# Hybrid decoder layer: rotary rows of the second key tile loaded with the first head, the last two gate stores moved to ScalarE, and another count of transfers in the planner

## The chip, the cores and the metric

The kernel runs on one core of a Trainium2 chip. The metric is the time of one execution on the device, in microseconds; the median of three runs stands for a kernel. The core has TensorE (PE) for matrix products, VectorE (DVE), ScalarE (ACT) and GpSimd (POOL) for elementwise work, SyncE (SP), which only issues transfers here, and 16 DMA engines. Each engine works through its own instructions in the order in which they were emitted, and waits at an instruction whose semaphores are not there yet.

## The reference

One layer of a decoder with 1024 tokens, 16 learned meta tokens in front, and 1024 channels. Cut to its core:

```python
h = rms_norm(h_res, pre_norm_g)
z = h @ w_in                       # 1024 -> 7328 columns: all branches, their gates, four merge gates
y_a = (pool_mixer(...) * silu(pg)) @ w_out_pool
y_b = (mla_attention(cq, ckv, kr, ...) * silu(mg)) @ w_out_mla
y_c = (conformer_conv(...) * silu(cg)) @ w_out_conf
y_d = (short_conv(...) * silu(sg)) @ w_out_sc
gts = sigmoid(gl + gate_bias)      # four gates of 1024 channels per token
m = gts[0]*y_a + gts[1]*y_b + gts[2]*y_c + gts[3]*y_d
out = h_res + rms_norm(m @ w_o, post_norm_g)
```

Attention has 8 heads. A key has 64 components of its own head and 32 rotary components, which are the same for every head (`k_rope` is broadcast). Values have 64 components.

## The kernel before

**Three stages.** Stage one is the input projection (with the convolutions, the norms and the attention's low-rank projections woven in); it ends with the 32 tiles of merge gates, which are written to DRAM as `th0` to `th31`. Stage two is attention, 8 heads by 2 halves of the queries, with the products of the other three branches (`fills`) as filling work. Stage three is the attention's output product and the product with `w_o`. Every operand of a product is kept as a high and a low part, and each product is made of three.

**The planner.** The code doesn't issue instructions directly: `PE`, `ACT`, `DVE`, `POOL` and `SP` record operations in a `Plan`, and `flush` puts the operations of one stage in an order by simulating them with assumed costs. An operation is ready when its dependencies have ended; among the ready ones of an engine, the lowest `prio` goes first (its place in the recording, less what `ahead` adds; the filling products are recorded with `plan.ahead(-400)`, so they come 400 places later). `behind` makes operations wait, in the plan alone, until the product of TensorE that was recorded last has ended. The start of an operation on SP or ScalarE that is a transfer also needs `fits`: with eight or more transfers in the list `landed`, the eighth last must have landed. Transfers of POOL are not in that list. A buffer gets a slot when its first operation starts; the slots of stage two lie on memory that stage one used, and each is free only when its last user there is done.

**Flushes.** `flush` is called once for each stage, and emits its whole order before the next stage is recorded. Each engine goes on, in the plan, from where it stood: SP, whose last operation of stage one is early, plans stage two's loads from there.

**Completion of transfers.** In the built program the transfers that SP and ScalarE issue (622 in all) add to eight semaphores, in turn; before a transfer is issued, its engine waits until all earlier transfers on the same semaphore are complete, that is, also the one eight places ahead in the program. POOL's two transfers use other semaphores.

**The gate stores.** `out_gate(g)` makes two tiles of gates, `th{g}` and `th{g+1}`, and stores each with ScalarE; for the last pair, `g == 30`, with POOL.

**The start of stage two.** POOL makes the masks `maskS`, `maskT`, the tile `negd`, and row 96 to 99 of both key tiles `kt[0]` and `kt[1]`. Heads alternate between these two tiles and between `vt[0]` and `vt[1]`. `load_kv(h)` loads the 64 key rows of a head and its values; the 32 rotary rows go once into each tile, with head 0 into `kt[0]` and with head 1 into `kt[1]`. `maxima(h, c)` makes the scores once to take each query's maximum (VectorE adds the mask and reduces; the result goes into the query tile's rows 96 to 99), and `attend(h, c)` makes them again, transposed, with the maximum subtracted, for the exponential on ScalarE and the split on POOL, and then the product with the values. At the beginning `load_q(0, 0)`, `load_kv(0)`, `load_q(0, 1)` and the first maxima are recorded; then, for each unit `i`, under `plan.behind()`, the loads of the query after next and of the next head.

**Filling work.** Each filling product needs `bo` (a branch's output, two tiles), `whl` (weights) and, for its eviction, `th` (a gate tile).

Of the kernel before, what the change touches and what calls it, by code (L numbers as in the profile page):

```python
# [14 lines left out]

# [49 lines left out]
def f(ap):  # L65
    return ap.bitcast(F32)
# [127 lines left out]
class Plan:  # L194
# [139 lines left out]
    def flush(self):  # L334
# [26 lines left out]
        def slot(b, t):  # L361

            free = [sl for sl in b.group["slots"] if not sl["live"] and sl["after"] <= t]
            if free and (b.group["any"] or b.group["order"][b.group["next"]] is b):
                return min(free, key=lambda sl: (sl["after"], sl["i"]))

        def fits(o, t):

            if o["op"] == "dma_start" and o["eng"] != "POOL" and len(self.landed) >= 8 and self.landed[-8] > t:
                return False  # L370
            return all(slot(b, t) for b in o["bufs"] if not b.live and b.group)

        while events:
            t = events[0][0]
            while events and events[0][0] <= t:
                _, kind, i = heapq.heappop(events)
                if kind == 0:
                    o = self.ops[i]
                    bisect.insort(ready[o["eng"]], (o["prio"], o["i"]))
                elif kind == 2:  # L380
                    for b in self.ops[i]["bufs"]:
                        b.left -= 1
                        if b.left == 0 and b.group:
                            b.slot["live"], b.slot["after"] = None, t
            for e in self.free:
                if self.free[e] > t:
                    continue
                o = next((self.ops[i] for _, i in ready[e] if fits(self.ops[i], t)), None)
                if o is None:
                    if e == "PE" and self.idle and self.ops[self.idle[1]]["end"] is None:  # L390
                        order.append(self.idle[0])
                        self.free[e] = t + 160
                        heapq.heappush(events, (self.free[e], 1, 0))
                    continue
                ready[e].remove((o["prio"], o["i"]))
                for b in o["bufs"]:
                    if not b.live:
                        b.live = True
                        if b.group:
                            b.slot = slot(b, t)  # L400
                            b.slot["live"] = b
                            b.group["next"] += 1
                o["start"] = t
                if o["turns"]:
                    o["cost"] += max(0, self.port[{"DVE": "POOL", "POOL": "DVE"}[e]] - t) * 0.7
                    self.port[e] = t + o["cost"]
                self.free[e] = t + o["cost"]
                o["end"] = t + o["cost"] + self.WAKE[e]
                if o["op"] == "dma_start":
                    if self.pipe is None:  # L410
                        self.pipe = max((x["done"] for x in self.ops if x["op"] == "dma_start"
                                         and "done" in x and x["start"] <= t), default=0)
                    o["done"] = self.pipe = max(self.pipe, t) + o["bytes"]
                    land = self.pipe + o["bytes"] + 4500 + min(0, o["extra"])
                    o["end"] = land + max(0, o["extra"])
                    if o["eng"] != "POOL":
                        self.landed.append(land)
                    heapq.heappush(events, (land, 1, 0))
                for b in o["bufs"]:
                    b.last = max(b.last, o["end"])  # L420
                order.append(o)
                heapq.heappush(events, (self.free[e], 1, 0))
                heapq.heappush(events, (o["end"], 2, o["i"]))
                for u in o["users"]:
                    u["need"] -= 1
                    same = u["eng"] == e and o["op"] != "dma_start"
                    u["at"] = max(u["at"], self.free[e] if same else o["end"])
                    if not u["need"]:
                        heapq.heappush(events, (u["at"], 0, u["i"]))
# [8 lines left out]
def trunk_kernel(ctx, tc, a):  # L438
    nc = tc.nc
    plan = Plan(nc)  # L440
    PE, ACT, DVE, POOL, SP = (plan.engine(e) for e in ("PE", "ACT", "DVE", "POOL", "SP"))
# [7 lines left out]
    def ld(out, in_):  # L449
        SP.dma_start(f(out) if out.dtype == F32R else out, f(in_) if in_.dtype == F32R else in_)  # L450
# [38 lines left out]
    th_dram = [dram.tile([P, NT], F32, name=f"th{i}") for i in range(32)]  # L489
# [6 lines left out]
    kr_dram = dram.tile([32, 2, L], F32R, name="kr")  # L496
# [136 lines left out]
    def full(to, x, ps):  # L633

        if x is None:
            copy(to, ps)
        else:
            add(DVE, to, ps, x)

    def pairs_of_halves(n, each, store):  # L640

        z = {}

        def out(i, j, ps, x, tmp):
            first = i not in z
            if first:
                z[i] = up.tile([P, 2, n], F32, tag="z", bufs=2, name="z")
            m = ps.shape[0]
            each(i, z[i][:m, j], ps, x, tmp)
            if not first:  # L650
                store(i, z[i][:m])
        return out
# [11 lines left out]
    def row(t):  # L664
        return t.rearrange("p j n -> p (j n)")
# [16 lines left out]
    def out_gate(g):  # L682

        def each(i, to, ps, x, tmp):
            if x is not None:
                full(to, x, ps)
            ACT.activation(to, ps if x is None else to, AF.Tanh, scale=0.5,
                           bias=par[:, R_GB + g + i:R_GB + g + i + 1])
        return pairs_of_halves(512, each, lambda i, t: (POOL if g == 30 else ACT).dma_start(th_dram[g + i], row(t)))

# [587 lines left out]
    def load_q(h, c):  # L1280
        qt[h, c] = qk.tile([NA, 2, 512], F32R, tag="q", bufs=3, name="qt")
        ld(qt[h, c][:QK].rearrange("p s n -> p (s n)"), q_dram[c][h].rearrange("p s n -> p (s n)"))

    load_q(0, 0)
    kt = [qk.tile([NA, 2, L], F32R, name=f"kt{i}") for i in range(2)]
# [4 lines left out]
    def load_kv(h):  # L1290
        e, k_, v_ = h % 2, kt[h % 2], vt[h % 2]
        ld(k_[:64].rearrange("p s n -> p (s n)"), k_dram[h // 2][64 * e:64 * (e + 1)].rearrange("p s n -> p (s n)"))
        if h == 0:
            ld(k_[64:96], kr_dram)
        if h == 1:
            ld(k_[64:80], kr_dram[16:])
            ld(k_[80:96], kr_dram[:16])
        v = v_dram[h // 4][h % 4]
        ld(v_[:, 0:8].rearrange("p j c -> p (j c)"), v[:, 0:8].rearrange("p j c -> p (j c)"))
        ld(v_[:NM, 8], v[:NM, 8])  # L1300
# [91 lines left out]
    op, smg = {}, {}  # L1392
# [58 lines left out]
    def refill():  # L1451
        count["u"] += 1
        while count["f"] < min(48, 48 * count["u"] / (NUNIT - 2)):

            with plan.ahead(-400):
                next(fill, None)
            count["f"] += 1
# [9 lines left out]
    def lead_to(i, n=0):  # L1467

        while lead["i"] <= min(i, len(seq) - 1) or lead["steps"] < n:
            if next(steps, "end") == "end":  # L1470
                lead["steps"] = math.inf
            lead["steps"] += 1

    load_kv(0)
    load_q(*seq[1])
    lead_to(0)
    units = 0
    for i, (h, c) in enumerate(seq):
        with plan.behind():
            if i + 2 < len(seq):  # L1480
                load_q(*seq[i + 2])
            if c == 0 and h + 1 < H:
                load_kv(h + 1)
            if c == 0 and h % 2:
                smg[h] = at.tile([P, NT], F32, tag="smg", name="smg")
                ld(smg[h], z_dram[f"mg{h // 2}"])
        for _ in attend(h, c):
            units += 1
            lead_to(-1, min(5 + units * 10 / 14, 5 * (i + 3)))
            refill()  # L1490
        lead_to(i + 1)
        with plan.ahead(-300):
            if h == H - 1:
                head_out(h, c, sums_pe(h, c))
            elif c:
                for k, rb in enumerate(sums(h)):
                    head_out(h, k, rb)
# [82 lines left out]
    for d in (0, 4, 1, 5, 2, 6, 3, 7):  # L1580
# [3 lines left out]
        for c in range(2):  # L1584
            t = th[:, 512 * c:512 * (c + 1)]
# [23 lines left out]
    def half(name, bufs=4):  # L1609
        return ep.tile([P, 512], F32, tag=name, bufs=bufs, name=name)  # L1610
# [71 lines left out]
    for t in range(4):  # L1682

        parts = [slice(0, 512)] if t < 3 else [slice(0, 256), slice(256, 512)]
        g = half("g", 1) if t == 3 else a_[t]
# [45 lines left out]
```

## Time and profile before

| | us |
|---|---|
| median of three runs (1006.8 to 1009.5) | 1008.29 |
| profiled execution, time | 1008.78 |
| profiled execution, span | 1007.1 |
| TensorE busy | 983.7 |
| GpSimd busy | 688.1 |
| VectorE busy | 685.0 |
| ScalarE busy | 448.3 |

The mean granted clock of TensorE is 0.994. All operations have one line in the profile, that of the helper which issues them (L332), so groups are told apart by the names of their tiles: `ps_pa` to `ps_pd` are the projection, `ps_s` scores and maxima, `ps_o` the product with the values, `ps_y` the filling products, `ps_u` and `ps_o` late in the span the last stage. `SPq` and `ACTq` are the queues in which SP and ScalarE issue transfers; `PEclk` is the granted clock.

### The profile page before, as it was taken

How to read it: one execution, taken by the hardware profiler on the slowest of the kernel's cores; microseconds unless marked ns; L12 is line 12 of the kernel's file. 1: busy time of each engine (PE TensorE's matmuls, PEld its weight loads, DVE VectorE, ACT ScalarE, POOL GpSimd, SP SyncE). 2: the span in 40 equal slices, each digit the busy share in tenths (PEclk: the TensorE clock that was granted, in tenths of full speed). 3: DMA queues.
4: the chain of work that ended last, by engine and by line, in shares of the span. 5: the costliest groups of instructions: out<-in, count | busy, mean ns of one | idle time of the engine just before them, and what ended most of it. 6: DMA issues, size and time to landing. Idle time of an engine off the chain costs nothing.

```text
span 1007.1 us, 15176 instructions
## 1 busy us (share of the span) xinstructions
PE 983.7 (98%) x5091; PEld 826.2 (82%) x5091; DVE 685.0 (68%) x1106; ACT 448.3 (45%) x895; POOL 688.1 (68%) x640
## 2 busy tenths in 40 slices
PE   9999999999999999999999999989999999999996
PEld 8999898889888878887877888868887878688885
DVE  5855695997899499444455453266677698598747
ACT  7633234443444545444444444215664655424632
POOL 6767876766777668667777676124588785846956
PEclk9999999999999999999999999999999999999998
DMA  7268756678775865766655556895757771572634
GB/s 248 76 219 281 247 169 190 194 244 294 242 248 186 283 215 177 241 176 191 204 178 187 175 167 167 293 267 161 235 175 224 212 232 54 209 242 72 207 118 167
DMA packets 126302, 203.13 MB, mean 202 GB/s; under 512 B 19650, under 2 KB 79161, under 8 KB 124880
## 3 DMA queue, kind: packets, MB, share of 16 engines
q1 hardware_dynamic: 121600, 185.38, 58.6%
q10 hardware_dynamic: 4336, 15.73, 4.2%
q8 instruction: 40, 0.66, 0.3%
q0 software_dynamic: 288, 1.05, 0.3%
q14 instruction: 38, 0.31, 0.1%
HBM read 128.40 MB, written 73.72 MB: 201 GB/s over the span
## 4 chain that ended last, share of the span: by engine, by line
PE 90%; DVE 4%; issue 2%; POOL 2%; DMA 1%; ACT 0%; SPq 0%; DVEq 0%; POOLq 0%; ACTq 0%
PE ps_pa L332 16%; PE ps_pb L332 16%; PE ps_pc L332 15%; PE ps_o L332 9%; PE ps_pd L332 8%; PE ps_u L332 7%; PE ps_s L332 7%; PE ps_y L332 6%; PE ps_x L332 4%; PE ps_w L332 1%; DMA kt<-kr 1%; POOL pt L332 1%; DVE mx L332 1%; DVE a L332 1%; DVE op L332 0%
## 5 line engine op out<-in xcount | busy, mean ns | idle before, releaser
L332 PE MATMUL ps_pb<-T,S 128*128 128x512 f32 (+2 forms) x792 | 172.4, 362 | 0.8 <-DVE u L332 0.8
L332 PE MATMUL ps_pa<-B,A 128*128 128x512 f32 (+2 forms) x792 | 172.2, 362 | 0.0
L332 POOL TENSOR_TENSOR S<-ss,S 128x512 fp32r<-128x512 f32 x84 | 110.5, 1328 | 77.2 <-ACT S L332 77.0
L332 PEld LDWEIGHTS ps_pa<-B,A 128*128 128x128 f32 x792 | 134.6, 188 | 24.4 <-issue 0.5
L332 PEld LDWEIGHTS ps_pb<-T,S 128*128 128x128 f32 x792 | 133.8, 188 | 24.4 <-DVE u L332 1.2
L332 POOL TENSOR_TENSOR A<-raw,A 128x512 fp32r<-128x512 f32 x84 | 117.0, 1398 | 48.2 <-ACT A L332 42.2
L332 POOL TENSOR_TENSOR pt<-p,pt 128x512 fp32r<-128x512 f32 (+4 forms) x112 | 106.1, 976 | 41.6 <-ACT pt L332 27.8
L332 ACT ACTIVATE S<-ss 128x512 fp32r<-128x512 f32 x84 | 50.8, 628 | 115.7 <-DVE ss L332 73.0
L332 PE MATMUL ps_y<-bo,whl 128*128 128x512 f32 x288 | 87.9, 410 | 1.3 <-DVE th L332 1.3
L332 DVE SCALAR_TENSOR_TENSOR ps_w<-conv,par,ps_w 128x512 f32<-128x512 f32 x116 | 87.2, 752 | 2.4
L332 PE MATMUL ps_pc<-B,S 128*128 128x512 f32 (+2 forms) x396 | 87.5, 364 | 0.5 <-DVE z L332 0.5
L332 PE MATMUL ps_pc<-T,S 128*128 128x512 f32 (+2 forms) x396 | 86.4, 363 | 0.4 <-DVE z L332 0.4
L332 ACT ACTIVATE p<-ps_s 128x512 f32<-128x512 f32 (+4 forms) x112 | 49.9, 446 | 82.1 <-DVE ps_s L332 30.9
L332 PE MATMUL ps_pd<-T,A 128*128 128x512 f32 (+2 forms) x396 | 84.9, 361 | 0.0
L332 PEld LDWEIGHTS ps_pc<-T,S 128*128 128x128 f32 x396 | 67.1, 188 | 13.2 <-issue 1.0
L332 PEld LDWEIGHTS ps_pc<-B,S 128*128 128x128 f32 x396 | 66.9, 188 | 13.2 <-issue 1.0
L332 PE MATMUL ps_o<-pt,vt 128*128 128x512 f32 (+4 forms) x336 | 76.2, 332 | 0.8 <-POOL pt L332 0.6
L332 PEld LDWEIGHTS ps_pd<-T,A 128*128 128x128 f32 x396 | 66.9, 188 | 11.9
L332 PE MATMUL ps_s<-qt,kt 100*128 100x512 f32 (+4 forms) x336 | 71.9, 333 | 2.1 <-DVE qt L332 2.1
L332 ACT ACTIVATE A<-raw 128x512 fp32r<-128x512 f32 x84 | 52.7, 627 | 37.0 <-PE ps_pd L332 23.0
L332 PEld LDWEIGHTS ps_s<-qt,kt 100*128 100x128 f32 x336 | 56.6, 184 | 14.7 <-DVE qt L332 3.4
L332 PEld LDWEIGHTS ps_o<-pt,vt 128*128 128x128 f32 x336 | 52.7, 174 | 13.3 <-POOL pt L332 2.3
(344 smaller groups left out, 1895.1 us busy)
## 6 DMA issues: line engine op xcount, KB each, us to landing
raw<-in_w_in_dram SPq DMA_DIRECT2D x56, 512.0 KB
th<-th SPq DMA_DIRECT2D x32, 512.0 KB
th<-z ACTq DMA_DIRECT2D x30, 512.0 KB
v<-vhl SPq DMA_DIRECT2D x16, 384.0 KB
qt<-q SPq DMA_DIRECT2D x16, 384.0 KB
vt<-v SPq DMA_DIRECT2D x8, 768.0 KB
bo<-bo SPq DMA_DIRECT2D x6, 1024.0 KB
kt<-k SPq DMA_DIRECT2D x8, 520.0 KB
```

The costliest lines, as they stand in the source:

```text
L332: getattr(self.handle[o["eng"]], o["op"])(*map(real, o["args"]), **{k: real(v) for k, v in o["kw"].items()})
```

## The change

```diff
         def fits(o, t):
-            if o["op"] == "dma_start" and o["eng"] != "POOL" and len(self.landed) >= 8 and self.landed[-8] > t:
+            if o["op"] == "dma_start" and o["eng"] != "POOL" and sum(s <= t < e for s, e in self.landed[-40:]) >= 8:
                 return False
...
                     if o["eng"] != "POOL":
-                        self.landed.append(land)
+                        self.landed.append((t, land))
...
-        return pairs_of_halves(512, each, lambda i, t: (POOL if g == 30 else ACT).dma_start(th_dram[g + i], row(t)))
+        return pairs_of_halves(512, each, lambda i, t: ACT.dma_start(th_dram[g + i], row(t)))
...
         if h == 0:
             ld(k_[64:96], kr_dram)
-        if h == 1:
-            ld(k_[64:80], kr_dram[16:])
-            ld(k_[80:96], kr_dram[:16])
+            ld(kt[1][64:80], kr_dram[16:])
+            ld(kt[1][80:96], kr_dram[:16])
...
     for i, (h, c) in enumerate(seq):
-        with plan.behind():
+        with plan.behind() if i else nullcontext():
             if i + 2 < len(seq):
                 load_q(*seq[i + 2])
```

The limit of eight now counts the transfers that have started and not landed at the time in question, among the last 40. The stores of `th30` and `th31` are issued by ScalarE. The rotary rows of `kt[1]`, two transfers of 130 KB, are loaded in `load_kv(0)`. The loads that are recorded at the first unit, the query of head 1 and head 1's keys and values, no longer wait in the plan for the last recorded product.

More of the change, by code (lines that the diff above doesn't have):

```diff
@@ L13 @@
 import re
-from contextlib import ExitStack, contextmanager
+from contextlib import ExitStack, contextmanager, nullcontext
 import concourse.bass as bass
```

## The prediction

> **What bounds the kernel now.** I read the page first: TensorE is busy nearly the whole span, so a change can only give back, or take, time in which it idles or runs below full clock.
>
> ```profile
> PE 983.7 (98%) x5091; PEld 826.2 (82%) x5091; DVE 685.0 (68%) x1106; ACT 448.3 (45%) x895; POOL 688.1 (68%) x640
> ```
>
> 1007.1 - 983.7 leaves 23.4 us of idle. The change works at the join of projection and attention, so next comes the chain of waits there, and then the stretches around it.
>
> ```profile
> 653.23 10.28 PE ps_y L332 x44
> ...
> 666.42 10.27 DMA kt<-kr
> ```
>
> ```profile
> 660.00:670.00 10.00, 9.19 (x41) 7.04 (x41) 7.67 (x20) 0.00 (x0) 0.11 (x1) 1.00 0.91 266
> 670.00:680.00 10.00, 7.66 (x37) 6.17 (x36) 5.67 (x16) 4.38 (x11) 3.76 (x6) 0.84 0.96 248
> ```
>
> ```profile
> 676.00:678.00 2.00, 1.18 (x5) 1.21 (x6) 0.61 (x2) 0.00 (x0) 0.00 (x0) 0.71 1.06 376
> 678.00:680.00 2.00, 2.00 (x9) 1.69 (x9) 0.00 (x1) 0.60 (x1) 0.00 (x0) 0.50 0.77 154
> 680.00:682.00 2.00, 2.00 (x7) 1.62 (x6) 1.42 (x4) 0.00 (x0) 0.00 (x0) 0.50 0.19 70
> 682.00:684.00 2.00, 2.00 (x7) 1.57 (x6) 1.62 (x4) 0.00 (x0) 0.00 (x0) 0.58 0.00 0
> ```
>
> In the stretches the first number pair is TensorE; the last three numbers are granted clock, DMA share and GB/s. TensorE fills the start of attention with branch products (`ps_y`) and then waits for the second key tile's rotary rows. The idle time is 0.81 + 2.34 = 3.15 us. The clock loss is 2 x (0.29 + 0.50 + 0.50 + 0.42) = 3.4 us. So this join costs 6.6 us: the most that closing the hole can bring.
>
> Why does attention start late? The timelines of GpSimd, TensorE and VectorE:
>
> ```profile
> 633.10 1.29 POOL L332 TENSOR_TENSOR S<-ss,S 128x512 fp32r<-128x512 f32 x1 [1.48 <-ACT S L332]
> 650.76 0.77 POOL L332 DMA_DIRECT2D th<-z  x1 [16.38 <-ACT z L332]
> 653.55 0.54 POOL L332 DMA_DIRECT2D th<-z  x1 [2.02 <-ACT z L332]
> 654.08 0.22 POOL L332 MEMSET maskS<- 128x128 f32 x1
> ...
> 658.33 0.16 POOL L332 MEMSET mx<- 128x12 f32 x2
> ```
>
> ```profile
> 651.59 0.58 PE L332 MATMUL ps_s<-kt,qt 96*128 96x144 f32 x3
> 652.01 1.10 PE L332 MATMUL ps_y<-bo,whl 128*128 128x512 f32 x4
> ...
> 668.50 1.95 PE L332 MATMUL ps_s<-qt,kt 100*128 100x512 f32 x9 [0.34 <-DVE qt L332]
> ```
>
> ```profile
> 664.14 1.47 DVE L332 TENSOR_REDUCE mx<-ps_s 128x1 f32<-128x144 f32 x4
> ```
>
> GpSimd waits 16.4 us to issue the last two gate stores and only then builds the masks and clears `mx`. VectorE's maxima therefore come at 664.14, and the first scores with an exponent (100 rows) at 668.50. The branch products keep TensorE busy meanwhile, because their operands have landed by 652.01. That cover is what I ask about next. The timeline of the transfers, SyncE with ScalarE's two stores:
>
> ```profile
> 631.03 0.33 ACTq L332 DMA_DIRECT2D th<-z  x1
> 633.81 0.33 ACTq L332 DMA_DIRECT2D th<-z  x1
> ```
>
> ```profile
> 614.41 0.42 SPq L332 DMA_DIRECT2D qt<-q  x1
> 614.88 0.51 SPq L332 DMA_DIRECT2D kt<-k  x1
> 615.79 1.52 SPq L332 DMA_DIRECT2D kt<-kr  x1
> 619.07 0.30 SPq L332 DMA_DIRECT2D qt<-q  x1
> 631.64 1.02 SPq L332 DMA_DIRECT2D whl<-w_out_pool  x2
> ```
>
> ```profile
> 634.41 0.32 SPq L332 DMA_DIRECT2D vt<-v  x1
> ```
>
> ```profile
> 638.11 0.32 SPq L332 DMA_DIRECT2D vt<-v  x1
> 638.53 0.37 SPq L332 DMA_DIRECT2D bo<-bo  x1
> ```
>
> ```profile
> SPq L332 <- DMA th<-z: 4.6, 2, 3.4
> ```
>
> The last row is from the grouped waits of SyncE's queue between 612 and 640. A load of attention values has nothing to do with a gate store, and yet it waits for two of them. The reason is in the program: transfers of SyncE and ScalarE take eight completion semaphores in turn, and each waits until the one eight places ahead has landed. Loads 1 to 6 of the second stage went out by 632.7; load 7 (`vt`, 634.41) is eight places behind ScalarE's store of 631.03, load 8 (638.11) behind that of 633.81. So these stores held SyncE 3.4 and 4.3 us after their issue. GpSimd's last two stores use other semaphores and hold nobody.
>
> **The change part by part.** The sum is made against the profiled execution, span 1007.1 and time 1008.78 us, 0.5 above the median of 1008.29.
>
> 1. *Two stores to ScalarE.* ScalarE issues them for 2 x 0.33 us, with nothing behind it until the first exponential: cost 0. GpSimd loses its 16.38 us wait and can build masks from 634.4, where its last split ends. VectorE can then take the maxima when the first scores arrive, at about 653, and the exponent scores could come some 5 us later instead of at 668.50. That is the gain, if keys, values and branch operands are there. The price: the stores now take two of the turns, just before the second stage's loads. They go out at about 650.8 and 653.6 as before, because the activations that feed them don't move. With the 3.4 and 4.3 us above they land at about 654.5 and 657.5. Counted in turns, load 5 now waits for the store of 631.03 (634.4), load 6 for that of 633.81 (638.1), load 7 for about 654.5, and load 8 (or 9, if a load stands between the two stores) for about 657.5. SyncE is one queue: whatever is behind them waits too.
>
> 2. *Transfers counted by their times.* The planner's old rule looked at the eighth last transfer in the list, landed or planned, and so held loads back as the turns do. The new one counts only those already started. It lets the planner put more loads ahead on paper; the turns don't follow the planner. Within a stage, where every listed transfer has started, both count nearly the same: 0, with 1 us either way for small shifts of order.
>
> 3. *Rotary rows early; no fence at the first unit.* Head 1's keys, values and queries get a place ahead of the branch loads, since the branch loads have 400 added to their order. Sizes from the transfers' view:
>
> ```profile
> bo<-bo SPq DMA_DIRECT2D x6, 1024.0 KB
> ...
> vt<-v SPq DMA_DIRECT2D x8, 768.0 KB
> ```
>
> Two queries, keys and rotary rows of both heads make about eight loads, whose buffers are free early. So the first values, the branch operands `bo` and the branch weights come at or behind load 9, that is after 657.5. Ahead of the second `bo`: values of two heads 2 x 780 KB, two weights 512 KB, two `bo` 2048 KB, in all 4120 KB or 4.2 MB. The rate of saturated stretches:
>
> ```profile
> 642.00:646.00 4.00, 4.00 (x19) 3.25 (x18) 1.38 (x2) 0.73 (x1) 0.00 (x0) 1.00 0.99 357
> 646.00:650.00 4.00, 4.00 (x19) 3.22 (x18) 0.69 (x1) 0.96 (x2) 0.00 (x0) 1.00 1.01 382
> ```
>
> At 370 GB/s this takes 11.4 us, plus about 2 us to land (3.4 us for a store of 0.52 MB, less 1.4 at that rate): 671. If `bo` stands right behind load 9, 2.1 MB need 5.7 + 2: 665.
>
> *The cover that is gone.* After the projection TensorE has three or four maxima products and then branch products: in the order of before the first `ps_y` is the fourth instruction, at 652.01. TensorE keeps its order, so from about 653 it stands at that product until 665 to 671: 12 to 18 us, and I take 15, between both positions of `bo`. All else of attention stands behind. Then it restarts at reduced clock: the row of before gives 3.4 us. By the Trainium skill (TensorE: Matmul & The Clock Gate, Part 1) half clock comes after an idle window of about 3.4 us and ends after as long a busy one, which would make the restart 1.7 us; the row above, half clock after a wait of 2.2 us, differs from it, and I keep the row. By the skill the sum below would be 1.7 us lower.
>
> *Given back later.* Fewer branch products are used up before the attention starts, so more are left to fill its later holes. The largest of these:
>
> ```profile
> 860.00:880.00 20.00, 17.58 (x86) 12.98 (x85) 10.46 (x16) 6.85 (x15) 15.69 (x14) 1.00 0.75 261
> ```
>
> It holds 2.42 us of idle; bounds 0 and 2.4, I take 0.6, as products were left there in before too.
>
> Sum: -6.6 (old hole) + 15 + 3.4 - 0.6 = +11.2, from 1008.78 to about 1020. Low end: -6.6 + 12 + 1.5 (restart within a shorter low-clock stretch) - 2.4 = +4.5, 1013. High end: -6.6 + 18 + 3.4 + 2 (gate tiles `th` come behind `bo` and hold evictions) = +16.8, 1025.6.
>
> **The rivals.**
>
> *The hole closes (faster).* If the second stage's loads take their turns before the two stores, or SyncE has all of its early loads out by then, nothing waits. For it: SyncE issued nothing between 619.4 and 631.6, and DMA stood still in part of that time:
>
> ```profile
> 626.00:630.00 4.00, 4.00 (x19) 3.26 (x18) 1.00 (x2) 1.76 (x4) 1.30 (x1) 1.00 0.02 6
> ```
>
> Against it: the stores belong to the stage that is emitted first, and in the program of before the first load stands between GpSimd's two stores, not ahead of both. Time: 1008.78 - 6.6 + 1 for new order = 1003. The Trainium skill says the same by another way (DMA: Bandwidth & Descriptors, "Issuing engines are not separate DMA queues"): all issuers share the DMA engines, and a change of issuer saves only issue time. No row of before contradicts that on the transfers; the wait of 4.6 us above lies in front of the issue, which the rule doesn't count.
>
> *SyncE is held, but the order on TensorE has attention first (about the same).* If scores of the first unit stand ahead of the first branch product, TensorE works on maxima and scores until about 658 and idles some 6 us until values land near 661 to 663. Then -6.6 + 6 + 3.4 - 1 = +1.8: 1010. Against it: in before a branch product follows the third maxima product. It decides between this and my forecast whether the planner believes in operands at 652, and it does.
>
> *The change does nothing at the join.* The loads' order is set by buffers that come free at 631 to 641, the rotary rows land early but another load is waited for. Then 1008. The count by times alone, without the turns, could do this. I give it little.
>
> **How the numbers follow.** SyncE held and TensorE standing at the first branch product: 0.66, time 1013 to 1026, likeliest 1020. Hole closes: 0.19, 1001 to 1005. SyncE held but covered: 0.10, 1006 to 1013. Nothing: 0.05, 1006 to 1010. What a measurement of this kernel can tell from no change is about 0.3%, 3 us: 1005.3 to 1011.3. Faster gets 0.19; same 0.11 (0.05, and most of the 0.10); slower 0.70. The range for 8 in 10 must reach below the likeliest case's own 1013 to 1026, through the middle cases and into the faster one: 1003 to 1026.
>
> **What would show it.** GpSimd's mask rows move to about 635, and the `th<-z` rows stand on ScalarE's queue at about 650.5 and 653.3: these I expect in any case. Held: SyncE's queue has a gap that ends at about 654 and 657 with the releaser `DMA th<-z`, and `bo<-bo` is issued after 657; DMA share falls to near zero between 642 and 650, where it was 0.99; TensorE idles over 10 us with the releaser `DMA bo<-bo` and the clock goes to 0.5. Wrong: `bo<-bo` still at about 638 to 641, exponent scores near 658, clock at 1.00 from 650 to 700; then the stores' turns came after the loads.

## The result and the profile after

The changed kernel takes 1024.45 us (median of 4 runs, 1023.62 to 1024.52), the kernel before beside it 1008.89 (1006.80 to 1012.09): ratio 1.0149, 95% interval 1.0121 to 1.0178. The profiled execution has a span of 1022.7 us, 15.6 more than before, and a mean clock of 0.984 instead of 0.994.

The page's row of busy times, of the changed kernel:

```profile
PE 986.8 (96%) x5091; PEld 829.4 (81%) x5091; DVE 683.3 (67%) x1106; ACT 446.6 (44%) x895; POOL 688.2 (67%) x638
```

The same 5091 products were busy for 3.1 us more, and 1022.7 - 986.8 = 35.9 us were idle instead of 23.4. So 12.5 us of the 15.6 are standing still; the other 3.1 are the same products running longer, and the mean clock fell with them. The stretches around the join show where (pairs in the order TensorE, weight loads, VectorE, ScalarE, GpSimd; then clock, DMA share, GB/s):

```profile
640.00:650.00 10.00, 10.00 (x45) 8.13 (x44) 2.08 (x3) 2.05 (x3) 0.16 (x2) 1.00 0.04 11
650.00:660.00 10.00, 1.80 (x9) 1.27 (x8) 2.63 (x7) 0.81 (x2) 0.00 (x0) 0.78 0.76 232
660.00:670.00 10.00, 1.49 (x3) 0.83 (x3) 0.00 (x0) 0.00 (x0) 0.00 (x0) 0.50 1.00 386
670.00:680.00 10.00, 7.29 (x26) 5.54 (x26) 5.01 (x13) 0.07 (x1) 0.11 (x1) 0.70 0.65 238
```

First the DMA engines stand still for 10 us beside a busy TensorE (share 0.04, where it was 0.96 in the same ten microseconds before), and then TensorE stands still for almost 20 us beside busy DMA engines. From 640 to 680 TensorE idles 40 - 20.58 = 19.4 us; before it was 3.15. TensorE's timeline names what it waits for, in brackets:

```profile
651.22 0.58 PE L332 MATMUL ps_s<-kt,qt 96*128 96x144 f32 x3
668.51 1.65 PE L332 MATMUL ps_y<-bo,whl 128*128 128x512 f32 x3 [16.72 <-DMA bo<-bo]
672.32 0.80 PE L332 MATMUL ps_y<-bo,whl 128*128 128x512 f32 x1 [2.15 <-DMA bo<-bo]
...
678.39 1.96 PE L332 MATMUL ps_s<-qt,kt 100*128 100x512 f32 x9 [0.33 <-DVE qt L332]
```

Three products for the maxima, then the first branch product, 16.72 us without its operand, and 2.15 more for the operand's second tile. The exponent scores come at 678.39, ten microseconds later than before. SyncE's and ScalarE's queues, and the grouped waits of SyncE's queue from 610 to 680 (total, times, longest):

```profile
650.12 0.33 ACTq L332 DMA_DIRECT2D th<-z  x1
652.90 0.33 ACTq L332 DMA_DIRECT2D th<-z  x1
```

```profile
639.06 13.99 SPq L332 DMA_DIRECT2D kt<-kr  x2
653.10 0.48 SPq L332 DMA_DIRECT2D kt<-k  x1
656.64 0.82 SPq L332 DMA_DIRECT2D whl<-w_out_pool  x2
657.56 1.79 SPq L332 DMA_DIRECT2D vt<-v  x4
659.44 1.00 SPq L332 DMA_DIRECT2D bo<-bo  x1
...
661.36 0.59 SPq L332 DMA_DIRECT2D bo<-bo  x1
```

```profile
SPq L332 <- DMA th<-z: 33.5, 4, 13.4
```

Neighbours of one kind are one row: the second rotary load of the row at 639.06 went out at 652.75, after a wait for the store of 650.12, and the first branch weight at 656.64, after one for that of 652.90. Both branch operands follow behind. GpSimd meanwhile has its masks made early, to no use:

```profile
635.64 0.20 POOL L332 MEMSET maskS<- 128x128 f32 x1
```

### The profile page after: what moved, and what is told of

Read it like the earlier page. It is cut to its first block, busy times and chain, and to the rows that moved or that the text cites. A ratio compares the mean times of both kernels' runs of the same rounds, so it can differ in the third digit from the quotient of the medians.

```text
span 1022.7 us, 15174 instructions
## 1 busy us (share of the span) xinstructions
PE 986.8 (96%) x5091; PEld 829.4 (81%) x5091; DVE 683.3 (67%) x1106; ACT 446.6 (44%) x895; POOL 688.2 (67%) x638
## 4 chain that ended last, share of the span: by engine, by line
PE 92%; DVE 4%; DMA 1%; issue 1%; ACT 1%; SPq 0%; POOL 0%; DVEq 0%; ACTq 0%; POOLq 0%
PE ps_pb L332 16%; PE ps_pa L332 16%; PE ps_pc L332 15%; PE ps_o L332 10%; PE ps_y L332 8%; PE ps_s L332 8%; PE ps_pd L332 7%; PE ps_u L332 7%; PE ps_x L332 4%; DMA bo<-bo 1%; PE ps_w L332 1%; DVE ps_w L332 1%; DVE a L332 1%; SPq L332 0%; DVE ss L332 0%
## 5 line engine op out<-in xcount | busy, mean ns | idle before, releaser
L332 POOL TENSOR_TENSOR S<-ss,S 128x512 fp32r<-128x512 f32 x84 | 113.5, 1363 | 74.6 <-ACT S L332 69.2
L332 PEld LDWEIGHTS ps_pa<-B,A 128*128 128x128 f32 x792 | 134.5, 188 | 23.4
L332 POOL TENSOR_TENSOR pt<-p,pt 128x512 fp32r<-128x512 f32 (+4 forms) x112 | 103.3, 947 | 45.4 <-ACT pt L332 34.4
L332 PE MATMUL ps_y<-bo,whl 128*128 128x512 f32 x288 | 89.2, 415 | 19.8 <-DMA bo<-bo 18.9
L332 PEld LDWEIGHTS ps_y<-bo,whl 128*128 128x128 f32 x288 | 52.3, 195 | 29.7 <-DMA bo<-bo 19.9
L332 PE MATMUL ps_o<-pt,vt 128*128 128x512 f32 (+5 forms) x336 | 76.0, 330 | 0.1
L332 PE MATMUL ps_s<-qt,kt 100*128 100x512 f32 (+4 forms) x336 | 74.8, 339 | 0.5 <-DVE qt L332 0.3
L332 DVE TENSOR_REDUCE mx<-ps_s 128x1 f32<-128x144 f32 (+6 forms) x112 | 56.0, 508 | 26.8 <-PE ps_s L332 22.5
```

What stands on the lines that cost most here:

```text
L332: getattr(self.handle[o["eng"]], o["op"])(*map(real, o["args"]), **{k: real(v) for k, v in o["kw"].items()})
```

## The experiments

Ratios are to the kernel before, run in turns with it on the same chip; each has its 95% interval. "Old count" is the planner's rule of before, "new count" that of the change.

### One part undone: a1, the stores back on GpSimd

```diff
-        return pairs_of_halves(512, each, lambda i, t: ACT.dma_start(th_dram[g + i], row(t)))
+        return pairs_of_halves(512, each, lambda i, t: (POOL if g == 30 else ACT).dma_start(th_dram[g + i], row(t)))
```

> The changed kernel with the last two gate stores given back to GpSimd; all else as changed. Theory (the two stores' turns hold SyncE's loads): no wait of SyncE for th<-z after 638.5, bo issued near 640 and landed near 652, no idle of TensorE over 2 us at the join; the rotary rows of head 1 are early, so the old hole is gone too: 1003 us (1000 to 1009). Rival (the new order of the loads, with head 1's in front of the branch operands, is what starves TensorE): the branch operands stay late and the time stays above 1017 us.

Measured: 1010.19 us, 1.0019 [1.0007, 1.0032]; 14 us of the loss are gone, though 1 us more stays than the top of my range. The planner still puts the branch product fourth. SyncE is held for 16.2 us by the two earlier stores only, and the second tile of `bo`, behind head 1's loads, goes out at 644.11; TensorE waits 2.94 us for it:

```profile
655.43 0.80 PE L332 MATMUL ps_y<-bo,whl 128*128 128x512 f32 x1 [2.94 <-DMA bo<-bo]
```

In b1 below, which is a1 with rows and fence as before, that tile goes out at 639.77 and nothing waits for it.

### One part undone: a3, the old count

```diff
-            if o["op"] == "dma_start" and o["eng"] != "POOL" and sum(s <= t < e for s, e in self.landed[-40:]) >= 8:
+            if o["op"] == "dma_start" and o["eng"] != "POOL" and len(self.landed) >= 8 and self.landed[-8] > t:
...
-                        self.landed.append((t, land))
+                        self.landed.append(land)
```

> The changed kernel with the planner's old count of transfers. Theory (turns): SyncE is held as in the changed kernel, with the same two releases near 654.5 and 657.5, but the plan expects it and puts work that is there first: 1011 to 1018 us, between before and changed. If the count by times were what makes the loads late in the chip's order, this would be 1003 to 1008 us.

Measured: 1012.03 us, 1.0032 [1.0019, 1.0045]. This is the surprise against my prediction, which gave the count 0: it carries 12 us as the stores carry 14. SyncE is held as long as in the changed kernel, but TensorE has another order (grouped waits of SyncE's queue; TensorE's timeline, its first branch product):

```profile
SPq L332 <- DMA th<-z: 35.5, 5, 15.2
```

```profile
659.12 4.38 PE L332 MATMUL ps_s<-qt,kt 100*128 100x512 f32 x15 [0.87 <-DVE qt L332]
...
674.21 0.63 PE L332 MATMUL ps_y<-bo,whl 128*128 128x512 f32 x1
```

The edit is to the planner alone, and what it changes is the order. The reason can be read in the code: the old rule looks at the entry eight places back in `landed`, a list of the transfers of SyncE and ScalarE in the order in which they are emitted, across the two stages. That is the very transfer for which the built program waits. With the old count the planner therefore takes `bo` to be late and puts attention ahead of the branch products.

### One part alone: a2, only the stores (old count, rows and fence as before)

The edit is the store line of the change, in the kernel before.

> The kernel before with only the last two gate stores given to ScalarE (old count, rotary rows with head 1, fence kept). Theory (turns): SyncE is held at the seventh load to about 654.5 and at the ninth to about 657.5, the branch operands land near 668; the old count knows of it, so TensorE is given attention first and idles less than in the changed kernel: 1010 to 1016 us. Rival (order of loads alone): as before, 1008 us, or 1002 us because the masks are early.

Measured: 1006.92 us, 0.9985 [0.9976, 0.9994]: a miss, and on the other side of zero. SyncE is held for 36.6 us, yet the first values went out ahead of the longest of these waits (16.0), and the first branch product stands at 675.72:

```profile
SPq L332 <- DMA th<-z: 36.6, 5, 16.0
```

```profile
635.57 2.63 SPq L332 DMA_DIRECT2D vt<-v  x2
```

```profile
658.97 3.30 PE L332 MATMUL ps_s<-qt,kt 100*128 100x512 f32 x9
...
675.72 0.63 PE L332 MATMUL ps_y<-bo,whl 128*128 128x512 f32 x2
```

Here a held queue costs nothing, since TensorE's order doesn't ask for what is in it. With the masks early and attention ahead in that order, the exponent scores come at 658.97 instead of 668.50. Some of the gain is lost to the clock, which is 0.59 from 660 to 670.

### One part alone: b1, only the count

> The kernel before with only the count of transfers by their times (stores of the last pair on GpSimd, rotary rows with head 1, fence kept). Theory (the count only hurts where the turns hold loads that the plan takes for started): GpSimd's stores take no turns, so nothing more is held than before: SyncE waits for th<-z 8 us or less in all, bo is issued by 641, 1006 to 1011 us. If the count by itself puts loads in a bad order: above 1012 us.

Measured: 1005.64 us, 0.9960 [0.9939, 0.9982]: a gain of 4 us, just outside my range. `bo` goes out at 637.79, before any late turn, and the wait for the second tile's rotary rows shrinks from 2.2 to 0.22 us (TensorE's timeline); the join runs at full clock (20 us stretch):

```profile
637.79 0.37 SPq L332 DMA_DIRECT2D bo<-bo  x1
```

```profile
673.98 0.30 PE L332 MATMUL ps_s<-kt,qt 96*128 96x144 f32 x1 [0.22 <-DMA kt<-kr]
```

```profile
660.00:680.00 20.00, 18.80 (x93) 14.71 (x92) 16.09 (x41) 6.17 (x15) 4.34 (x8) 1.00 0.87 249
```

Most of the old hole closes without the other two parts. The earlier issue is not what closes it: the rows go out 0.9 us earlier than before (664.73 instead of 665.62), but TensorE too is there 0.9 us earlier, since its first stage ends that much sooner. What is shorter is the landing of the second load of rows, 8.50 us from issue instead of 10.27. Why it landed sooner stays open.

### One part alone: b2, rotary rows early and no fence (old count, stores on GpSimd)

> The kernel before with only the rotary rows of head 1 early and no fence at the first unit (old count, stores of the last pair on GpSimd). Theory: head 1's queries, keys and values (1.9 MB) now stand ahead of the branch operands, which land some 3 to 5 us later, about when TensorE wants them: the old hole of 6.6 us at the join goes, a wait of TensorE for bo of 1 to 4 us comes, with a low clock after it: 1005 to 1011 us. Rival (the early rows are the gain that was meant and nothing pays for it): 1001 to 1003 us.

Measured: 1013.38 us, 1.0039 [1.0018, 1.0060]: a miss, and the wait for `bo` that I expected isn't there. The profiled execution (1015.87 us) loses time in three places. At the join TensorE waits for no load; its gaps are of at most 0.47 us, behind VectorE. Yet the clock is 0.74 over 20 us, some 20 x 0.26 = 5.2 us, so the early rows take the old wait away and leave a loss of like size. In the middle of attention stands a new hole, with 2.5 us idle and some 20 x 0.25 = 5 us of clock:

```profile
660.00:680.00 20.00, 18.66 (x70) 15.28 (x70) 13.58 (x34) 3.84 (x10) 4.69 (x10) 0.74 0.59 221
820.00:840.00 20.00, 17.49 (x70) 14.05 (x69) 17.98 (x34) 8.45 (x19) 9.83 (x12) 0.75 0.44 140
```

And the first stage, whose text this edit doesn't touch, ends 2.4 us later than in the profile of before (its last group of twelve products starts at 651.19 instead of 648.81). Some 1.8 us of that are clock: TensorE waits 1.1 us at 363 in both, but behind it the clock is 0.91 in this execution and 1.00 in that of before (before, then b2):

```profile
360.00:380.00 20.00, 18.88 (x94) 15.49 (x93) 19.61 (x30) 10.50 (x19) 15.69 (x14) 1.00 0.44 146
360.00:380.00 20.00, 18.89 (x84) 15.23 (x83) 18.52 (x28) 9.89 (x19) 13.80 (x12) 0.91 0.47 156
```

The profiles of a2, a3 and c1 show 0.91 there too. So it is hardly an effect of the rows.

### Two parts: e1, the stores and the count, without rows and fence

> The kernel before with both last gate stores on ScalarE and the count by times, but rotary rows and fence as before: the pair that I hold for the cause, without the third part of the change. TensorE's order at the join is that of the changed kernel (fourth instruction a `ps_y`), while head 1's loads stand behind both `bo`. By turns, the first values then wait for the store of about 650 and the first `bo` for that of about 653, so `bo` goes out at about 656.7 as the store lands, two loads earlier than the 659.4 of the changed kernel and with 0.8 MB instead of some 2.7 MB under way ahead of it. If the pair holds TensorE and head 1's loads only lengthen it: `bo` lands at about 662 and its second tile at 664, the stall is 9 to 13 us instead of 18.9, and the time 1011 to 1019. Rival: all three parts are needed, because without head 1's loads `bo` is out before the held turn: stall under 3 us, 1003 to 1008. Rival: head 1's loads have no share in it: stall of 17 us or more, 1021 to 1026.

Measured: 1019.23 us, 1.0109 [1.0088, 1.0129], 0.2 us over my range; the stall is 12.24 + 2.12 = 14.4 us, over its 13. In part that is the second store, which took longer to land. The chain of waits has it with 6.17 us from issue, where that of the changed kernel has 3.67 (e1, then the changed kernel, then e1's SyncE queue; in e1 the values went out at 652.20, just before the store):

```profile
652.31 6.17 DMA th<-z
```

```profile
652.90 3.67 DMA th<-z
```

```profile
658.54 0.32 SPq L332 DMA_DIRECT2D bo<-bo  x1
...
659.43 0.38 SPq L332 DMA_DIRECT2D bo<-bo  x1
```

```profile
663.46 1.65 PE L332 MATMUL ps_y<-bo,whl 128*128 128x512 f32 x3 [12.24 <-DMA bo<-bo]
667.23 0.79 PE L332 MATMUL ps_y<-bo,whl 128*128 128x512 f32 x1 [2.12 <-DMA bo<-bo]
```

So the pair is enough for the stall, and head 1's loads ahead of `bo` make it 18.9 - 14.4 = 4.5 us longer. Rows and fence were only tried together; with them as one part, these are all eight combinations:

| rows and fence | stores | old count | new count |
|---|---|---|---|
| as before | GpSimd | 1 | 0.9960 |
| as before | ScalarE | 0.9985 | 1.0109 |
| as changed | GpSimd | 1.0039 | 1.0019 |
| as changed | ScalarE | 1.0032 | 1.0149 |

No part costs more than 0.4% alone. Only the stores and the count together cost over 1%, with the rows or without.

### Turns or bytes: a4, the stores on GpSimd and two tiny transfers on ScalarE

```diff
+    bit_dram = [dram.tile([P, 32], F32, name=f"bit{i}") for i in range(2)]
...
-        return pairs_of_halves(512, each, lambda i, t: ACT.dma_start(th_dram[g + i], row(t)))
+        def store(i, t):
+            (POOL if g == 30 else ACT).dma_start(th_dram[g + i], row(t))
+            if g == 30:
+                ACT.dma_start(bit_dram[i], row(t)[:, :32])
+        return pairs_of_halves(512, each, store)
```

Otherwise the changed kernel. The two transfers copy 16 KB each to a place that nobody reads.

> The changed kernel with the full gate stores on GpSimd, as in the first of this set, and beside them ScalarE copies 32 columns of each of the two gate tiles (16 KB) to a place that nobody reads: it adds two turns that end late and 32 KB of traffic, nothing else. Theory (turns): SyncE is held to about 653 and 656, the branch operands land near 669, 1019 to 1025 us like the changed kernel. Rival (the 1 MB of stored bytes in ScalarE's queue, or the bytes ahead of the branch operands): like the first of this set, 1000 to 1009 us.

Measured: 1024.60 us, 1.0162 [1.0144, 1.0181], as much as the changed kernel, with the gate stores where they were before:

```profile
SPq L332 <- DMA th<-z: 16.9, 2, 11.3
SPq L332 <- DMA bit<-z: 14.9, 2, 12.1
```

```profile
667.58 1.65 PE L332 MATMUL ps_y<-bo,whl 128*128 128x512 f32 x3 [15.38 <-DMA bo<-bo]
```

The only difference to a1 is two transfers of 16 KB, late, in the rotation of semaphores, and they cost 14.4 us. It is the turns and not the bytes. The Trainium skill says (DMA: Bandwidth & Descriptors, "Issuing engines are not separate DMA queues") that all issuers share the DMA engines and that another issuer only saves time on the sequencer. Of the transfers themselves nothing here contradicts that; the 14 us lie ahead of the issue, in a wait that the rule doesn't count.

### The stalled operand let past the queue: d2, `bo` and the first branch weights issued by GpSimd

```diff
-    def ld(out, in_):
-        SP.dma_start(f(out) if out.dtype == F32R else out, f(in_) if in_.dtype == F32R else in_)
+    def ld(out, in_, eng=None):
+        (eng or SP).dma_start(f(out) if out.dtype == F32R else out, f(in_) if in_.dtype == F32R else in_)
...
-                ld(t.rearrange("p s n -> p (s n)"), bo_dram[branches[bi][2] + k].rearrange("p s n -> p (s n)"))
+                ld(t.rearrange("p s n -> p (s n)"), bo_dram[branches[bi][2] + k].rearrange("p s n -> p (s n)"), POOL if bi == 0 else None)
...
+                eng = POOL if bi == 0 and d < 3 else None
-                whl = wtile(fp, wname, d, 0)
+                whl = wtile(fp, wname, d, 0, eng)
-                ld(th, th_dram[8 * gi + d])
+                ld(th, th_dram[8 * gi + d], eng)
```

> The changed kernel with the loads of the first branch (its two `bo` tiles and the first three pairs of `whl` and `th`) issued by GpSimd, whose transfers take none of the eight turns; ScalarE keeps the last two gate stores and the count stays. My theory: the loss at the join is TensorE standing at the first `ps_y` for `bo`, behind the held SyncE. Then SyncE is still held (`th<-z` some 30 us in all, values not before 655), but `bo` lands by 648 and TensorE works on branch products meanwhile: idle of the join under 3 us instead of 19.4, and 1003 to 1011. Rival: the held keys and values themselves are the loss; then TensorE runs out of branch weights (three pairs, about 9 us) near 662 and stands for values until 663 to 668, 3 to 8 us with the clock behind it: 1011 to 1018. Rival: the loss lies in the new order of later work (hole at 820 to 860); then 1018 or more.

Measured: 1010.43 us, 1.0009 [0.9997, 1.0022]. SyncE is held for 37.6 us, no less than in the changed kernel, but with `bo` out of its queue 14 us are won back and no branch product waits for it. The idle time of the join is 6.9 us and not under 3, for the held values come next, as the first rival had it:

```profile
666.99 0.77 PE L332 MATMUL ps_o<-pt,vt 128*128 128x512 f32 x1 [5.61 <-DMA vt<-v]
```

### The same in the kernel before: c1 with the old count, d1 with the new

Both have the stores on ScalarE and d2's edit, with rows and fence as before.

> The kernel before with the last two gate stores on ScalarE (as in the run of the stores alone, old count, fence and rotary rows as before) and the first branch's operands and the first three pairs of branch weights and gate tiles loaded by GpSimd, whose transfers take no part in the eight turns. Theory (turns are what keeps the branch operands away): bo is issued near 638 to 642, lands before 652, TensorE has branch products at the join while attention starts near 658: idle under 1.5 us between 640 and 680 and clock 1.00: 999 to 1004 us. Rival (the join is bound by the bytes to be loaded, whoever issues them): TensorE still idles 2 us or more there, 1005 to 1010 us.

> The kernel before with three edits: both last gate stores issued by ScalarE, the loads of the first branch issued by GpSimd, and the count by times; rotary rows and fence as before. With the old count this had a clean join but a first stage that ended 1.7 us later and holes of 2 to 5 us behind. If the count by times itself brings stage one's end to 651.5 or earlier, as in the three kernels here that have it without the first stage's late hole, the gains add: 1001 to 1005. Rival: gains don't add, since each new order opens holes of 2 to 5 us elsewhere: 1005 to 1009.

Measured: c1 1006.33 us, 0.9963 [0.9947, 0.9978]; d1 1010.48 us, 1.0011 [0.9996, 1.0026]. Both came out above the range of my theory, and d1 above that of its rival as well. The join of c1 is clean (1.0 us idle over 40 us, clock 1.00):

```profile
640.00:660.00 20.00, 19.23 (x84) 14.73 (x83) 8.57 (x20) 2.86 (x4) 4.96 (x12) 1.00 0.83 292
660.00:680.00 20.00, 19.81 (x106) 16.11 (x105) 13.38 (x38) 12.72 (x29) 12.10 (x14) 1.00 0.82 220
```

Its first stage ends 1.8 us later than in the profile of before (last group at 650.60 instead of 648.81), which is the clock of 0.91 at 360 to 380 again and not the price of the clean join. In d1 the first stage ends 0.85 us earlier (647.96), but the rotary rows of the second tile stand again behind the held turns, and TensorE meets them:

```profile
668.94 0.46 PE L332 MATMUL ps_s<-kt,qt 96*128 96x144 f32 x1 [3.56 <-DMA kt<-kr]
```

So both kinds of gain exist, but together they don't add. The fastest version measured is the new count alone, 0.9960; c1 is its equal within the intervals.

## Why the prediction was right, and which steps were not

The direction, the mechanism and the place came out: the stores' turns hold SyncE, `bo` is issued after 657, and TensorE stands at the first branch product. The signs named for "held" are all there: masks at 635.64 (about 635 forecast), stores at 650.12 and 652.90 (650.5 and 653.3), the queue's gaps ending at 652.75 and 656.64 (654 and 657), DMA share 0.04 from 640 to 650, clock 0.50. The places came out as counted, too: loads 5, 6, 7 and 9 of the second stage are the ones held, until 633.28, 639.06, 652.75 and 656.64. The terms of the sum:

| term | forecast, us | measured, us |
|---|---|---|
| old hole | -6.6 | -6.6 |
| stall at the first `ps_y` | +15 | +18.9 |
| other idle time at the join | 0 | +0.5 |
| restart at half clock | +3.4 | +2.7 |
| later: idle time given back | -0.6 | -3.8 |
| later: new hole's clock | 0 | +3.4 |
| sum | +11.2 | +15.1 (span +15.6) |

*The stall was mis-sized by 3.9 us.* I let TensorE arrive at 653 and took the middle, 668, for its end. It started to wait at 651.8, since only three products stand ahead; it went on at 668.51; and the second `bo` tile cost 2.15 us more, which my single figure had no place for. a1 and e1 bear the working out: without the two late turns 2.9 us, with the turns but without head 1's loads 14.4, with both 18.9.

*The restart* is read from the 2 us stretches: 0.5 x (1.49 + 0.16 + 1.68 + 2.00) = 2.7 us. Only the busy time counts here; in my 3.4 us for the row of before, the first stretch was taken as busy throughout, and with its 1.18 us the row gives 3.2.

```profile
668.00:670.00 2.00, 1.49 (x3) 0.83 (x3) 0.00 (x0) 0.00 (x0) 0.00 (x0) 0.50 1.02 428
670.00:672.00 2.00, 0.16 (x1) 0.00 (x0) 0.00 (x0) 0.00 (x0) 0.00 (x0) 0.50 1.00 395
672.00:674.00 2.00, 1.68 (x5) 1.41 (x6) 0.43 (x1) 0.00 (x0) 0.00 (x0) 0.50 1.04 401
674.00:676.00 2.00, 2.00 (x7) 1.72 (x6) 1.26 (x4) 0.00 (x0) 0.11 (x1) 0.50 0.66 258
```

*Given back later.* The join idles 19.4 - 3.15 = 16.3 us more and the whole span only 12.5, so idle time outside the join fell by 3.8 us, more than the 2.4 that I had as a bound. But a hole at 836, where TensorE waits 1.72 us for a maximum on VectorE, brought a clock loss that I had not foreseen, some 20 x 0.09 + 20 x 0.08 = 3.4 us:

```profile
820.00:840.00 20.00, 17.75 (x91) 14.43 (x90) 15.62 (x36) 7.78 (x21) 16.07 (x19) 0.91 0.72 224
840.00:860.00 20.00, 20.00 (x101) 16.80 (x100) 12.12 (x31) 12.39 (x28) 12.80 (x14) 0.92 0.15 44
```

The two nearly cancel, which is luck: neither was forecast in this size, and without one of them the sum would be off by as much again as the stall was. What makes that hole stays open. Other orders have their own: the clock from 820 to 840 is 0.83 in e1, 0.87 in c1 and 1.00 in b1.

*The step that was wrong is step 2.* It priced the count at 0, with 1 us either way, because "the turns don't follow the planner". That is so, and it is the point: the old count followed the turns for the planner. Within a stage the two counts may well agree, but the change acts between two stages. SyncE plans its loads from a time before the last gate stores start; the new count doesn't see these stores, and the old one did. With the old count the planner knew that `bo` would be late and put attention first (a2, a3), which is my second rival, "SyncE is held, but the order on TensorE has attention first". I rejected that rival by the order of before, in which a branch product follows the third maxima product. It was evidence of an order made while the queue was free. So what decides between forecast and rival is the count: 1.0149 with the new, 1.0032 with the old. The forecast held because the changed kernel has the new one, and not for the reason that I gave; this too is luck.

*The faster rival* came in another way than I had thought: with the count alone most of the old hole is gone (b1). I had put "the count alone" at about no change.

*One reading of before was too strong.* I put VectorE's late maxima down to GpSimd's late `mx`. But `mx` is cleared by 658.5, and the first maximum comes only at 664.14: until then VectorE, in its order, takes the branch products as they end. So the stores explain the time up to 658.5, and the order the rest:

```profile
663.53 0.69 DVE L332 SCALAR_TENSOR_TENSOR m<-th,ps_y 128x512 f32<-128x512 f32 x1 [0.71 <-PE ps_y L332]
```

## What to carry to other kernels

In a program built like this one, a transfer that is moved to another engine also moves into that engine's rotation of completion semaphores, and what stands eight places behind it, on any engine in the rotation, waits for its landing: count the places, not the bytes (two transfers of 16 KB cost 14.4 us in a4). A planner's rule that looks like a needless limit can be its only knowledge of a real one; when it goes, the planner orders work for operands that can't be there, and TensorE, which keeps its order, stands at them (16.72 us here). Time the parts of a change in all combinations before keeping or dropping one, since here each cost 0.4% at most and two together over 1%.

## What the runs showed of the hardware

The clock can fall without any long wait. In d2 TensorE had short gaps of at most 0.40 us, 1.29 us out of four, and then ran for about 2 x (0.44 + 0.42) / 0.5 = 3.4 us at half clock:

```profile
650.00:652.00 2.00, 1.63 (x8) 1.05 (x6) 0.96 (x3) 0.34 (x1) 0.00 (x0) 1.00 0.88 305
652.00:654.00 2.00, 1.08 (x4) 0.58 (x4) 1.93 (x7) 0.38 (x1) 0.00 (x0) 1.00 1.00 320
654.00:656.00 2.00, 2.00 (x7) 1.76 (x7) 1.90 (x7) 0.00 (x0) 0.11 (x1) 0.56 0.98 385
656.00:658.00 2.00, 2.00 (x8) 1.38 (x7) 0.96 (x3) 0.00 (x0) 0.00 (x0) 0.58 1.05 426
```

The Trainium skill (TensorE: Matmul & The Clock Gate, Part 1) has half clock after at least one idle window of about 3.4 us and full clock after a busy one. The length of the slow stretch agrees; that the window must be idle does not, for TensorE was busy for 2.71 of these first 4 us.

The slow stretch can also be much longer than these 3.4 us, beside a TensorE that the profile shows as busy. In a3, after waits of 2.32 and 0.87 us, the clock was 0.52 for a whole stretch of 20 us:

```profile
660.00:680.00 20.00, 19.58 (x59) 14.73 (x59) 11.30 (x31) 5.13 (x13) 3.83 (x7) 0.52 1.01 349
```

It is 59 products in 19.58 us, where b1 has 93, of another mix, in 18.80 at full clock, and costs some 20 x 0.48 = 9.6 us: more than half of what a3 wins by not standing at `bo`. The join of b2 is a case of both: after gaps of at most 0.47 us the clock is 0.74 over 20 us. What holds it down so long stays open.
